# A feed-forward layer with fewer seven-product blocks, and matmul operands at one rest of 512 bytes

## The chip, the cores and the metric

The kernel runs on one core of one Trainium2 chip. The time is that of the device, in microseconds (us), as the median of several runs. TensorE multiplies matrices, VectorE (DVE) and ScalarE (ACT) do elementwise work, GpSimd (POOL) does small vector work and issues some DMAs, and SyncE (SP) issues most loads. Each engine works through its own queue in order, and semaphores tie the queues together.

## The reference

Two layers over 256 frames of width 2048, in float32. Layer 0 has a gated linear attention as its mixer, layer 1 a sparse attention; each adds its output to x, and then a gated feed-forward layer adds its own. What the change touches is the latter:

```python
def swiglu(h, w1, w3, w2):
    return (jax.nn.silu(h @ w1) * (h @ w3)) @ w2

def reference(x, ...):
    for i in range(DEPTH):                      # 2
        h = rmsnorm(x, norm_mix[i])
        ...
        x = x + y
        x = x + swiglu(rmsnorm(x, norm_ffn[i]), ffn_w1[i], ffn_w3[i], ffn_w2[i])
    return rmsnorm(x, norm_final)
```

w1 and w3 are 2048 x 5632, w2 is 5632 x 2048.

## The kernel before

**Products in three passes.** A float32 operand is split into a high part in the float32r format and the remainder: ScalarE casts the high part (`wh`, line 135), VectorE subtracts it (`wl`, line 136). A product is hi·wh + hi·wl + lo·wh, three matmuls of a 128 x 128 stationary tile and a 128 x 512 moving tile. The stationary tiles come from the activations, the moving ones from the weights. Weights arrive in tiles of 128 x 2048 (1 MB): four slices of 128 rows, by 512 columns. One such tile against one set of stationary tiles is 4 x 3 = 12 matmuls for 128 frames.

**The feed-forward layer** (`ffn`) works through 11 blocks of 512 columns of w1 and w3. With the 256 frames as two halves and the 2048 rows as two halves, one block is two products (with w1 and with w3) of a 2 x 2 block matrix. There are two ways to compute it:

- `plain` takes four products of half size for each of w1 and w3, eight in all, of 24 matmuls each: 192 matmuls. Its eight weight tiles come through the `raw` buffers (four of them) and are split once each. It uses the forms A11, F7 (the half difference a21 - a11), A12 and N22 (the negative of a22) of the activations.
- `pair` computes the two 2 x 2 products, which share their left matrix, with seven products of half size: 168 matmuls. For this it needs sums of weight tiles. Some are made by VectorE (`plus`, line 405), others by a DMA that adds what it loads to what lies in the buffer (`plus_dma`, line 408, issued on POOL's queue). Each product splits its two tiles anew: 14 casts and 14 subtractions. The tiles that are summed lie in the buffers v0, v1, v2 and g3, used in two sets that change places with `turn`, which is `b // 2 % 2` for block b; SP loads them at line 380. The activations have seven forms (fhA11, flA11, ... in the trace `fhA`, `fhF`, `fhN` and `fl` alike, numbers left out). There the lines are 393 for matmuls of a pair and 463 for those of a plain block.

The forms A11, F7, F5, A12, F6, F3 and N22 are made once for a layer, by `NormF`.

Both ways end in `done`, which makes silu(h w1) times h w3 for a half of the frames: it begins with a tanh on ScalarE (line 512). `split_t` then transposes the result (eight small matmuls a block, line 215) and splits it into the tiles `g0`, `g1` or `g2`, which are the stationary operands of the product with w2.

**The product with w2** is cut up. After blocks 1, 3, 5 and 7 the two finished blocks are put on a queue `down` as a generator `pieces`: eight steps, each with one tile of w2 and 24 matmuls (lines 489 to 491). The next block's generator yields eight times if it is a pair, twice if it is plain, and at each yield one step of `down` is issued. A generator that has given its eight steps is taken off `down` only when it is asked once more. So after block 2, 4, 6 and 8 the queue still holds an emptied generator, and it is dropped at the first yield of block 3, 5, 7 and 9. Since a block is a pair `if down`, blocks 2 to 9 are pairs, those with even numbers with eight pieces between their products, those with odd numbers with none. Blocks 0, 1 and 10 are plain. Blocks 8, 9 and 10 are multiplied with w2 in the step that follows (`residual`).

The other projections run through `gemm` (lines 201 to 203): stationary hh and hl, the normed activations, or `g` for the output projections; the last one ends in `gemm_tail` (lines 152 to 154), whose first wh and wl come from a pool of its own, the last one opened.

**Order.** The program is issued in the order of the code; each engine takes its instructions in that order. POOL's adding DMAs of a pair are issued one by one.

**Where tiles lie.** Pools take SBUF in the order in which they are opened: `cst` (small constants), `res` (x and g0 to g3), `wp` (raw, wh, wl), `cm`, `sm` (small tiles, 32 bytes each at the least), and then one pool for each stage, which holds hh and hl (`gp`, `dp`) or the forms and v0 to v2 (`fz0`, `fz1`), or the pool of the last step (`fp`). `cst` begins at byte 2176 of each partition. `cst` holds 32 + 512 + 288 bytes, `sm` 46 slots of 32 bytes, one of them an unused tile named pad. All other pools ahead of the stage's pool take multiples of 512 bytes.

Of the kernel before, what the change touches and what calls it, by code (L numbers as in the profile page):

```python
# [12 lines left out]
F32 = mybir.dt.float32  # L13
# [6 lines left out]
P = 128  # L20
# [3 lines left out]
NB = 512  # L24
# [31 lines left out]
def trunk(  # L56
# [9 lines left out]
    cst = ctx.enter_context(tc.tile_pool(name="cst", bufs=1))  # L66
# [3 lines left out]
    sm = ctx.enter_context(tc.tile_pool(name="sm", bufs=2))  # L70
# [13 lines left out]
            nc.sync.dma_start(x[t][n], x2[t, :, n * NB:(n + 1) * NB])  # L84


    neghalf = cst.tile([P, 8], F32, name="neghalf")
    nc.gpsimd.memset(neghalf, -0.5)
    warm = sm.tile([P, 8], F32, tag="warm", bufs=1, name="warm")
# [4 lines left out]
    cols = cst.tile([P, 72], F32, name="cols")  # L94


    sm.tile([P, 8], F32, tag="pad", bufs=1, name="pad")

    def gains(c0, srcs):

# [14 lines left out]
    def tick():  # L115

        while side:
            try:
                return next(side[0])
            except StopIteration:  # L120
                side.popleft()
# [9 lines left out]
    def split_w(raw, pool=wp):  # L131

        wh = pool.tile([P, 4, NB], F32R, tag="wh", bufs=3 if pool is wp else 1, name="wh")
        wl = pool.tile([P, 4, NB], F32R, tag="wl", bufs=3 if pool is wp else 1, name="wl")
        nc.scalar.copy(wh, raw)  # L135
        nc.vector.tensor_sub(wl, raw, wh.bitcast(F32))  # L136
        return wh, wl
# [221 lines left out]
    def hi_lo(i):  # L359
        g = res.tile([P, 2, 4, SEQ], F32R, tag=f"g{i}", name=f"g{i}")  # L360
        return g[:, 0], g[:, 1]

    def flush():
        while side:
            tick()


    def pair(nrm, wa, wb, c0, turn, done):

        def src(w, j, c):
            r = j * 1024 + c * 512
            return w[r:r + 512, c0:c0 + NB].rearrange("(k p) n -> p k n", p=P)

        def load(w, j, homes):
            o = []
            for c, (pool, tag, bufs) in enumerate(homes):
                raw = pool.tile([P, 4, NB], F32, tag=tag, bufs=bufs, name=tag)
                nc.sync.dma_start(raw, src(w, j, c))  # L380
                o.append(raw)
            return o

        def product(acc, raws, form, start, stop, then=None):
            for c in range(2):
                wh, wl = split_w(raws[c])
                if then is not None:
                    then(c)
                hi, lo = nrm.forms[form]
                for j in range(4):  # L390
                    k = 4 * c + j
                    for i, (l_, r_) in enumerate(((hi, wh), (hi, wl), (lo, wh))):
                        nc.tensor.matmul(acc, l_[:, k, :], r_[:, j, :], start=start and k == i == 0,  # L393
                                         stop=stop and k == 7 and i == 2, skip_group_check=not start)
                    if j % 2:
                        tick()

        def bank():
            return acc_p.tile([P, NB], F32, tag="acc", name="acc")

        def sums(tag):
            return nrm.pool.tile([P, NB], F32, tag=tag, bufs=1, name=tag)

        def plus(dst, other):
            return lambda c: nc.vector.tensor_add(dst[c], dst[c], other[c])  # L405

        def plus_dma(dst, w, j):
            return lambda c: nc.gpsimd.dma_start(dst[c], src(w, j, c), accum_op=ALU.add)  # L408

        fz = nrm.pool  # L410
        stream = [(wp, "raw", RAW)] * 2
        homes = [((fz, "v0", 1), (fz, "v1", 1)), ((fz, "v2", 1), (res, "g3", 1))]
        va = load(wa, 0, homes[turn])
        vb = load(wb, 0, homes[1 - turn])
        b1 = bank()
        product(b1, va, "A11", True, True, plus(va, vb))
        s1 = sums("s1")
        nc.scalar.copy(s1, b1)
        yield
        b2 = bank()  # L420
        product(b2, va, "F5", True, True, plus_dma(va, wb, 1))
        y = sums("y")
        nc.vector.tensor_sub(y, b2, s1)
        yield
        vc = load(wb, 1, stream)
        product(b2, vc, "F3", False, True, plus(vb, vc))
        yield
        b3 = bank()
        product(b3, va, "F6", True, True, plus_dma(va, wa, 1))
        w = sums("w")  # L430
        nc.vector.tensor_sub(w, b3, s1)
        yield
        product(b3, vb, "F7", False, True)
        nc.vector.tensor_add(w, w, b2)
        nc.vector.tensor_add(y, y, b3)
        yield
        vd = load(wa, 1, stream)
        product(b1, vd, "A12", False, True)
        done("11", b1)
        done("12", w)  # L440
        yield
        product(b3, va, "N22", False, True)
        nc.vector.tensor_sub(s1, s1, b3)
        done("21", s1)
        done("22", y)
        yield
        yield

    def plain(nrm, ws, c0, done):

        for q, w in zip("12", ws):
            acc = [acc_p.tile([P, NB], F32, tag="acc", name="acc") for _ in range(3)]
            for g in range(4):
                raw = wp.tile([P, 4, NB], F32, tag="raw", bufs=RAW, name="raw")
                nc.sync.dma_start(raw, w[g * NB:(g + 1) * NB, c0:c0 + NB].rearrange("(k p) n -> p k n", p=P))
                wh, wl = split_w(raw)
                for bank, form, start, stop in ((0, "A11", True, True), (1, "F7", True, True)) if g < 2 else \
                        ((0, "A12", False, True), (2, "N22", True, True)):
                    hi, lo = nrm.forms[form]
                    for j in range(4):  # L460
                        k = 4 * (g % 2) + j
                        for i, (l_, r_) in enumerate(((hi, wh), (hi, wl), (lo, wh))):
                            nc.tensor.matmul(acc[bank], l_[:, k, :], r_[:, j, :], start=start and k == i == 0,  # L463
                                             stop=stop and k == 7 and i == 2, skip_group_check=not start)
                        if j % 2:
                            tick()
                if g == 1:
                    s1 = nrm.pool.tile([P, NB], F32, tag="s1", bufs=1, name="s1")
                    nc.scalar.copy(s1, acc[0])
                    nc.vector.tensor_add(s1, s1, acc[1])  # L470
                    yield
            nc.vector.tensor_sub(s1, s1, acc[2])
            done("1" + q, acc[0])
            done("2" + q, s1)
# [24 lines left out]
    def ffn(layer, nrm):  # L499

        w1, w3, w2 = ffn_w1[layer], ffn_w3[layer], ffn_w2[layer]
        sc = {}
        parts = []
        down = deque()
        for b in range(DFF // NB):
            us = [None] * NT

            def done(q, v):
                t = int(q[0]) - 1
                if q[1] == "1":  # L510
                    us[t] = cm.tile([P, NB], F32, tag="u", name="u")
                    nc.scalar.activation(us[t], v, AF.Tanh, scale=sc["h"][:, t:t + 1])
                    nc.vector.scalar_tensor_tensor(us[t], us[t], 1.0, v, op0=ALU.add, op1=ALU.mult)
                else:
                    nc.vector.scalar_tensor_tensor(us[t], us[t], sc["r2"][:, t:t + 1], v, op0=ALU.mult, op1=ALU.mult)

            for slot, _ in enumerate(pair(nrm, w1, w3, b * NB, b // 2 % 2, done) if down else plain(nrm, (w1, w3), b * NB, done)):
                if b == 0 and slot == 0:
                    flush()
                    r = nrm.rstd()  # L520
                    sc["h"] = scaled(r, 0.5, "rh")
                    sc["r2"] = sm.tile([P, NT], F32, tag="r2", name="r2")
                    nc.gpsimd.tensor_tensor(sc["r2"], r, sc["h"], op=ALU.mult)
                while down:
                    try:
                        next(down[0])
                        break
                    except StopIteration:
                        down.popleft()
            hi, lo = hi_lo(b % 3)  # L530
            side.append(split_t(us, hi, lo))
            parts.append((hi, lo, b * NB))
            if b % 2 and b < 8:
                down.append(pieces(w2, parts))
                parts = []
        while down:
            for _ in down.popleft():
                pass
        return w2, parts
# [480 lines left out]
    with tc.tile_pool(name="gp", bufs=2) as gp:  # L1020
        n0.begin(gp)
        down = gla(n0, gp)
        flush()
    with tc.tile_pool(name="fz0", bufs=1) as fz:
        n1.begin(fz)
        residual(gla_w_out[0], down, n1.update)
        down = ffn(0, n1)
        flush()
    with tc.tile_pool(name="dp", bufs=2) as dp:
# [3 lines left out]
        down = dsa(n2, dp)  # L1033
        flush()
    with tc.tile_pool(name="fz1", bufs=1) as fz:
        n3.begin(fz)
        residual(dsa_w_out[0], down, n3.update)
        down = ffn(1, n3)
# [57 lines left out]
```

## Time and profile before

| | |
|---|---|
| median of 3 runs | 2426.34 us (2423.76 to 2428.74) |
| the profiled execution, in all | 2430.86 us |
| its span, first to last instruction | 2429.1 us |
| mean granted TensorE clock | 0.973 |
| DMA, mean over the span | 203 GB/s |
| read from HBM | 489.59 MB |

How to read it: the span is a little shorter than the time of the same execution, since it leaves out what lies before the first and after the last instruction. Busy times of matmuls overlap, since each begins before the one before it has ended; so the mean duration of one (some 390 ns) isn't its cost in a row of matmuls. The distance between two starts is. In a row of the timeline stand start and duration in us, engine, line, operation, output and inputs, and in brackets the engine's idle time before it and what ended it. In a row of the table of windows stand the stretch, its length, the busy time and the number of instructions of each engine, the granted clock, the share of the DMA engines and GB/s.

### The profile page before, as it was taken

To read this page: it belongs to the slowest core of one execution; us is meant where nothing else is said; L and a number is where in the kernel's file an instruction comes from. 1 tells how busy PE (TensorE), PEld (TensorE's weight loads), DVE (VectorE), ACT (ScalarE), POOL (GpSimd) and SP (SyncE) were. 2 spreads that over 40 slices of the span, in tenths; PEclk is the share of its full clock that TensorE was granted. 3 is DMA by queue.
4 is the path that set the end of the run, shared out by engine and by line. 5 is a ranking of instruction groups with operands and counts; after the bars stand their busy time and mean duration, and the time that the engine had idled before them with its cause. 6 is when DMAs were issued, how large, how long until landed. Compare 5 with 4: busy or idle time off the path is not lost.

```text
span 2429.1 us, 25156 instructions
## 1 busy us (share of the span) xinstructions
PE 2281.5 (94%) x10199; PEld 1857.5 (76%) x10199; DVE 1645.9 (68%) x1348; ACT 1183.5 (49%) x1053; POOL 112.8 (5%) x159
## 2 busy tenths in 40 slices
PE   9999999998897979989999999999988979889798
PEld 7888888876675867768888888888876867768687
DVE  6555456677886878865556655565786778878754
ACT  5545455454454445544444454454444545545443
POOL 0000000000000000000100000000000000000000
PEclk9999999999999989999999999999998999989899
DMA  8555466586877968775554545566677977779663
GB/s 280 164 174 180 148 219 232 172 233 194 232 242 207 286 184 222 229 205 187 182 173 139 191 157 174 174 219 212 176 235 201 293 182 225 230 190 311 138 218 112
DMA packets 254773, 493.36 MB, mean 203 GB/s; under 512 B 8200, under 2 KB 20832, under 8 KB 254528
## 3 DMA queue, kind: packets, MB, share of 16 engines
q1 hardware_dynamic: 219856, 423.33, 51.1%
q0 software_dynamic: 33792, 67.11, 16.0%
q8 instruction: 80, 1.31, 0.2%
q10 hardware_dynamic: 1008, 1.31, 0.2%
q14 instruction: 37, 0.30, 0.0%
HBM read 489.59 MB, written 2.12 MB: 202 GB/s over the span
## 4 chain that ended last, share of the span: by engine, by line
PE 59%; issue 21%; DMA 9%; DVE 8%; ACT 2%; POOL 1%; SPq 0%; POOLq 0%; ACTq 0%; DVEq 0%
PE acc L201 11%; PE acc L203 11%; PE acc L202 11%; PE acc L463 10%; DMA g<-in_ffn_w 6%; PE acc L393 6%; DVE wl L136 5%; DMA v<-in_ffn_w 3%; PE down L490 2%; ACT wh L135 2%; PE down L491 2%; PE down L489 2%; DVE v L405 1%; POOL v L408 1%; PE trq L827 0%
## 5 line engine op out<-in xcount | busy, mean ns | idle before, releaser
L192 DVE TENSOR_TENSOR wl<-raw,wh 128x2048 fp32r<-128x2048 f32 (+3 forms) x161 | 350.1, 2176 | 314.8 <-ACT wh L191 314.6
L136 DVE TENSOR_TENSOR wl<-raw,wh 128x2048 fp32r<-128x2048 f32 x179 | 409.5, 2289 | 184.7 <-ACT wh L135 184.7
L135 ACT CAST wh<-raw 128x2048 fp32r<-128x2048 f32 x179 | 342.3, 1912 | 392.6 <-PE down L491 144.3
L191 ACT CAST wh<-raw 128x2048 fp32r<-128x2048 f32 (+3 forms) x161 | 291.9, 1815 | 278.8 <-PE acc L203 217.7
L136 DVE TENSOR_TENSOR wl<-v,wh 128x2048 fp32r<-128x2048 f32 x120 | 272.7, 2286 | 83.1 <-ACT wh L135 83.1
L201 PE MATMUL acc<-wh,hh 128*128 128x512 f32 (+3 forms) x832 | 327.1, 393 | 0.0
L135 ACT CAST wh<-v 128x2048 fp32r<-128x2048 f32 x120 | 227.4, 1904 | 198.9 <-DMA v<-in_ffn_w 99.9
L203 PE MATMUL acc<-wh,hl 128*128 128x512 f32 (+3 forms) x832 | 318.4, 383 | 0.0
L202 PE MATMUL acc<-wl,hh 128*128 128x512 f32 (+3 forms) x832 | 317.0, 381 | 0.5 <-DVE wl L192 0.5
L393 PE MATMUL acc<-wh,fhF 128*128 128x512 f32 x512 | 216.5, 426 | 59.3 <-ACT wh L135 59.2
L393 PE MATMUL acc<-wl,fhF 128*128 128x512 f32 x512 | 216.0, 422 | 30.9 <-DVE wl L136 30.9
L490 PE MATMUL down<-wl,g 128*128 128x512 f32 x512 | 204.0, 398 | 9.3 <-DVE wl L136 9.3
L393 PE MATMUL acc<-wh,flF 128*128 128x512 f32 x512 | 212.2, 414 | 0.0
L491 PE MATMUL down<-wh,g 128*128 128x512 f32 x512 | 202.9, 396 | 0.0
L489 PE MATMUL down<-wh,g 128*128 128x512 f32 x512 | 200.3, 394 | 0.0
L203 PEld LDWEIGHTS acc<-wh,hl 128*128 128x128 f32 x832 | 156.2, 188 | 30.8
L202 PEld LDWEIGHTS acc<-wl,hh 128*128 128x128 f32 x832 | 156.6, 188 | 30.3 <-issue 1.7
L201 PEld LDWEIGHTS acc<-wh,hh 128*128 128x128 f32 x832 | 156.5, 188 | 28.9 <-issue 1.9
L393 PEld LDWEIGHTS acc<-wh,fhF 128*128 128x128 f32 x512 | 103.9, 205 | 91.2 <-ACT wh L135 68.3
L201 PE MATMUL acc<-wh,g 128*128 128x512 f32 x424 | 167.2, 394 | 0.0
L203 PE MATMUL acc<-wh,g 128*128 128x512 f32 x424 | 165.5, 390 | 0.0
L202 PE MATMUL acc<-wl,g 128*128 128x512 f32 x424 | 165.4, 390 | 0.0
(282 smaller groups left out, 3608.6 us busy)
## 6 DMA issues: line engine op xcount, KB each, us to landing
raw<-in_ffn_w SPq DMA_DIRECT2D x200, 1024.0 KB, 5.8
v<-in_ffn_w SPq DMA_DIRECT2D x48, 1024.0 KB, 6.6
v<-in_ffn_w POOLq DMA_DIRECT2D x48, 1024.0 KB, 9.4
raw<-in_dsa_w_in SPq DMA_DIRECT2D x48, 1024.0 KB, 5.1
raw<-in_gla_w_in SPq DMA_DIRECT2D x40, 1024.0 KB, 5.1
raw<-in_gla_w_out SPq DMA_DIRECT2D x16, 1024.0 KB, 5.2
g<-in_ffn_w SPq DMA_DIRECT2D x16, 1024.0 KB, 6.7
g<-in_ffn_w POOLq DMA_DIRECT2D x16, 1024.0 KB, 13.3
```

Of the source, the lines that this page charges most:

```text
L135: nc.scalar.copy(wh, raw)
L136: nc.vector.tensor_sub(wl, raw, wh.bitcast(F32))
L191: a = nc.scalar.copy(wh[:, sl, :n], raw[:, sl, :n])
L192: v = nc.vector.tensor_sub(wl[:, sl, :n], raw[:, sl, :n], wh[:, sl, :n].bitcast(F32))
L201: nc.tensor.matmul(acc[t][:, :n], hi[:, k, ts_], wh[:, k, :n], start=start, stop=False)
L202: nc.tensor.matmul(acc[t][:, :n], hi[:, k, ts_], wl[:, k, :n], start=False, stop=False)
L203: nc.tensor.matmul(acc[t][:, :n], lo[:, k, ts_], wh[:, k, :n], start=False, stop=last)
L393: nc.tensor.matmul(acc, l_[:, k, :], r_[:, j, :], start=start and k == i == 0, stop=stop and k == 7 and i == 2, skip_group_check=not start)
L463: nc.tensor.matmul(acc[bank], l_[:, k, :], r_[:, j, :], start=start and k == i == 0, stop=stop and k == 7 and i == 2, skip_group_check=not ...
L489: nc.tensor.matmul(acc[t], hi[:, k, ts_], wh[:, k, :], start=start, stop=False)
L490: nc.tensor.matmul(acc[t], hi[:, k, ts_], wl[:, k, :], start=False, stop=False)
L491: nc.tensor.matmul(acc[t], lo[:, k, ts_], wh[:, k, :], start=False, stop=last)
```

## The change

The choice between `pair` and `plain` no longer asks whether `down` holds a generator but goes by the number of the block: 2, 4, 6 and 8 are pairs, and 0, 1, 3, 5, 7, 9 and 10 are plain. In addition an unused tile of 64 bytes is put first into `cst`, and the unused tile of `sm` grows from 32 to 96 bytes, so that tiles behind the first move by 64 bytes and tiles behind both by 128.

```diff
@@ -84,6 +84,7 @@
             nc.sync.dma_start(x[t][n], x2[t, :, n * NB:(n + 1) * NB])
 
 
+    cst.tile([P, 16], F32, name="pad")
     neghalf = cst.tile([P, 8], F32, name="neghalf")
     nc.gpsimd.memset(neghalf, -0.5)
     warm = sm.tile([P, 8], F32, tag="warm", bufs=1, name="warm")
@@ -94,7 +95,7 @@
     cols = cst.tile([P, 72], F32, name="cols")
 
 
-    sm.tile([P, 8], F32, tag="pad", bufs=1, name="pad")
+    sm.tile([P, 24], F32, tag="pad", bufs=1, name="pad")
 
     def gains(c0, srcs):
 
@@ -514,7 +515,7 @@
                 else:
                     nc.vector.scalar_tensor_tensor(us[t], us[t], sc["r2"][:, t:t + 1], v, op0=ALU.mult, op1=ALU.mult)
 
-            for slot, _ in enumerate(pair(nrm, w1, w3, b * NB, b // 2 % 2, done) if down else plain(nrm, (w1, w3), b * NB, done)):
+            for slot, _ in enumerate(pair(nrm, w1, w3, b * NB, b // 2 % 2, done) if b in range(2, 9, 2) else plain(nrm, (w1, w3), b * NB, done)):
                 if b == 0 and slot == 0:
                     flush()
                     r = nrm.rstd()
```

## The prediction

> **What bounds the kernel now.** I read the page first, then the ACT timeline for marks that part the blocks of the feed-forward layer, then the table of windows between these marks.
>
> ```profile
> span 2429.1 us, 25156 instructions
> ...
> PE 2281.5 (94%) x10199; PEld 1857.5 (76%) x10199; DVE 1645.9 (68%) x1348; ACT 1183.5 (49%) x1053; POOL 112.8 (5%) x159
> ```
>
> TensorE is busy for 94% of the span, so the kernel is bound by matmuls almost everywhere. The question is where the other 6% lies, and what one matmul costs.
>
> My mark is the first tanh of a block (line 512, reading an accumulator). That of block 1 in layer 0 is
>
> ```profile
> 461.40 0.69 ACT L512 ACTIVATE u<-acc,rh 128x512 f32<-128x512 f32 x1 [0.84 <-PE acc L463]
> ```
>
> and the windows run from such a mark to another. Layer 0 is the rows from 416.60 to 1092.36, layer 1 those from 1694.08 on.
>
> ```profile
> core 0: us, PE busy (x) PEld busy (x) DVE busy (x) ACT busy (x) POOL busy (x), PEclk, DMA share, GB/s
> 416.60:461.40 44.80, 44.80 (x201) 36.81 (x200) 24.85 (x19) 18.95 (x15) 0.00 (x0) 1.00 0.60 188
> 461.40:549.46 88.06, 86.23 (x381) 70.49 (x380) 66.92 (x43) 43.28 (x27) 5.41 (x4) 1.00 0.75 212
> 549.46:625.52 76.06, 62.96 (x260) 49.57 (x258) 55.33 (x36) 34.90 (x22) 5.17 (x4) 0.93 0.77 212
> 625.52:696.59 71.07, 65.54 (x285) 52.74 (x286) 61.41 (x39) 38.94 (x25) 5.19 (x4) 1.00 0.86 247
> 696.59:844.48 147.89, 129.03 (x545) 102.28 (x544) 116.67 (x75) 73.61 (x47) 10.37 (x8) 0.97 0.81 226
> 844.48:993.51 149.03, 131.12 (x545) 104.60 (x544) 117.10 (x75) 73.81 (x46) 10.38 (x8) 0.94 0.81 229
> 993.51:1066.60 73.09, 60.83 (x249) 47.98 (x248) 56.20 (x37) 34.99 (x23) 5.19 (x4) 0.93 0.71 186
> 1066.60:1092.36 25.76, 25.76 (x117) 21.05 (x116) 18.60 (x15) 14.34 (x11) 0.00 (x0) 1.00 0.60 207
> ...
> 1694.08:1781.34 87.26, 86.10 (x381) 70.49 (x380) 66.91 (x43) 43.30 (x27) 5.23 (x4) 1.00 0.75 214
> 1781.34:1930.95 149.61, 133.02 (x545) 106.19 (x544) 116.93 (x75) 73.85 (x47) 10.37 (x8) 0.93 0.80 227
> 1930.95:2080.80 149.85, 132.89 (x545) 106.31 (x544) 116.91 (x75) 73.82 (x46) 10.37 (x8) 0.93 0.79 224
> 2080.80:2229.34 148.54, 132.24 (x545) 105.60 (x544) 117.11 (x75) 74.05 (x46) 10.37 (x8) 0.92 0.81 227
> 2229.34:2304.09 74.75, 62.23 (x249) 49.12 (x248) 56.27 (x37) 34.97 (x22) 5.18 (x4) 0.91 0.70 184
> 2304.09:2329.73 25.64, 25.64 (x117) 21.03 (x116) 18.67 (x15) 14.34 (x12) 0.00 (x0) 1.00 0.62 208
> ```
>
> Three kinds of block stand here. A plain block (first row, 192 matmuls and 8 transposes) has TensorE busy for all of its 44.80 us at full clock. A seven-product pair with the eight pieces of w2 between its products (second row, from block 1 into block 2) loses under 2 us of 88.06. A seven-product pair alone, block 3 (third row), loses 13 us, and the granted clock falls to 0.93. Block 9 alone (993.51 and 2229.34) loses 12 us in each layer. So the pairs without pieces, blocks 3, 5, 7, 9, hold the idle time. What happens in them:
>
> ```profile
> 589.96 1.90 ACT L135 CAST wh<-v 128x2048 fp32r<-128x2048 f32 x1 [5.68 <-DMA v<-in_ffn_w]
> 600.86 1.90 ACT L135 CAST wh<-g 128x2048 fp32r<-128x2048 f32 x1 [9.00 <-DMA g<-in_ffn_w]
> ```
> ```profile
> 591.91 1.22 PE L393 MATMUL acc<-wh,fhF 128*128 128x512 f32 x2 [6.88 <-ACT wh L135]
> ```
>
> The cast waits for the adding DMA of line 408, and TensorE waits for the cast. The pair has a chain of its own (cast, split, adding DMA, cast again), and with only 24 matmuls between two links nothing covers it. With pieces in between, it is covered.
>
> **The change, part by part.**
>
> *Blocks 3, 5, 7, 9 of both layers become plain.* Each goes from 7 products of 24 matmuls (168) to 192, so 8 x 24 = 192 matmuls are added. Per block, six casts and six splits go, four adds on VectorE, four adding DMAs on POOL's queue; SP issues eight loads in both forms. Of these, VectorE's splits are
>
> ```profile
> L136 DVE TENSOR_TENSOR wl<-v,wh 128x2048 fp32r<-128x2048 f32 x120 | 272.7, 2286 | 83.1 <-ACT wh L135 83.1
> ```
>
> 6 x 2.286 = 13.7 us a block, and the casts and adds come on top. I cost all of it at nothing: in the pair alone it lies beside TensorE's work or inside the chain whose wait is already in the old rows, and a plain block keeps VectorE busy for 24.85 of 44.80 us only. What counts is TensorE's time between marks, and three transitions make up the new layer.
>
> Plain into pair (blocks 1-2, 3-4, 5-6, 7-8): the trace has this one, 88.06 and 87.26, mean 87.66. The later ones issue in the same order. Each pair's first tiles are the buffers that the pair before released earliest, and now a whole plain block lies between; the loads of a pair stand on SP's queue behind the plain block's eight loads, as they do for block 2, whose first cast of such a tile waited for TensorE and not for a DMA:
>
> ```profile
> 475.13 1.91 ACT L135 CAST wh<-v 128x2048 fp32r<-128x2048 f32 x1 [2.16 <-PE acc L463]
> ```
>
> Pair into plain (2-3, 4-5, 6-7, 8-9): not in the trace. From mark to mark it has 24 matmuls of the last product, 72 of three pieces, 84 of the plain block, and 8 transposes. The row from 1066.60 (25.76; 25.64 in layer 1) is the same without the pieces and lost nothing. So 25.70 + 72 x 0.2269 (the pace is below) = 42.0. From below the bound is these matmuls, 41; from above the row into a pair alone, 76.06. I take 42.0, since the nearest row has a plain block behind a pair and TensorE busy throughout. The plain block's loads have four buffers and go out in the order in which they are used.
>
> Plain into plain (9-10): 44.80.
>
> New layer, mark of block 1 to mark of block 10: 4 x 87.66 + 4 x 42.0 + 44.80 = 563.4. Old: the rows of layer 0 add up to 630.96, of layer 1 to 635.65. Saved: 67.5 + 72.2 = **139.8 us**. The matmuls that are added are in this sum: they are 192 x 0.2288 = 44, so the idle time and lower clock that go are worth some 184.
>
> What is late next is the pair itself: block 2 keeps one wait of 1.8 us for its adding DMA, which is in the 87.66.
>
> *The pads.* The pools lie one behind the other: constants, residents (x, g), weights (wh, wl), work tiles, small tiles, then the layer's pool with hh or the fh/fl forms. Everything is a multiple of 512 bytes except the constants (832) and the small tiles (46 slots of 32 bytes, 1472 = 2 x 512 + 448). So g stands at the same rest of 512 as wh and wl, and hh, fh, fl stand 64 bytes behind. The pads make these pools 896 and 1536: all at one rest, and by the base of 2176 bytes that rest is 0. Does the rest matter? Four stretches of the PE timeline, 128x512 matmuls with nothing between:
>
> ```profile
> 380.21 0.39 PE L201 MATMUL acc<-wh,g 128*128 128x512 f32 x1
> ...
> 395.41 0.39 PE L202 MATMUL acc<-wl,g 128*128 128x512 f32 x1
> ```
> ```profile
> 410.16 0.39 PE L463 MATMUL acc<-wh,fhA 128*128 128x512 f32 x1
> ...
> 421.60 0.39 PE L463 MATMUL acc<-wh,flA 128*128 128x512 f32 x1
> ```
> ```profile
> 156.37 0.39 PE L201 MATMUL acc<-wh,hh 128*128 128x512 f32 x1
> ...
> 165.98 0.39 PE L201 MATMUL acc<-wh,hh 128*128 128x512 f32 x1
> ```
> ```profile
> 2404.16 0.39 PE L152 MATMUL acc<-wh,g 128*128 128x512 f32 x1
> ...
> 2406.73 0.39 PE L154 MATMUL acc<-wh,g 128*128 128x512 f32 x1
> ```
>
> The 67 steps with g take 15.20 us, 0.2269 each. The 50 with the forms take 11.44, the 42 with hh 9.61: 0.2288 each. The last has g again, but wh comes from the last pool, so that the rests differ the other way: 11 steps in 2.57, 0.2336. One line, one shape, one stationary tile, and the pace goes with the rests. So equal rests are worth about 1.9 ns a matmul. How many:
>
> ```profile
> L201 PE MATMUL acc<-wh,hh 128*128 128x512 f32 x736 | 296.8, 403 | 0.0
> ```
>
> Three such lines with hh make 2208; the forms after the change have 8 pairs x 168 + 14 plain x 192 = 4032. 6240 x 1.9 ns = **12 us**. No trace shows both at rest 0, so I keep both ends: no gain (0), and everything at the worst pace seen. The second is 6240 x 4.8 ns + 2880 matmuls with g x 6.7 ns = 49 us lost.
>
> The Trainium skill, TensorE: Matmul & The Clock Gate, Part 2 (what happens when you issue a matmul), gives TensorE two independent read ports and says that loading the next weights does not take read bandwidth from the running matmul; by that rule the pads are worth nothing. The steps of 0.2336 against 0.2269 speak against it, at least for how the two rests stand to each other.
>
> *Sum.* The profiled run took 2430.9 us in all (span 2429.1). 2430.9 - 139.8 - 12 = 2279. The median shown, 2426.3, lies 4.5 below that run, so the forecast is **2275 us**.
>
> **The rivals.**
>
> 1. *The rests are worth nothing.* Loads of weights and reads of the moving operand do not disturb one another, and the 0.2288 comes from something else in these stages. For it: 2 ns is little, and hh and the forms differ from g in more than their address. Against: the tail's 0.2336. 2275 + 12 = 2287.
> 2. *Rest 0 is a bad one.* Both operands on it meet at every matmul. 2275 + 12 + 49 = 2336. Against: g and wh agree now, at another rest, and that is the fastest pace.
> 3. *The adding DMA is late in pairs 4, 6, 8 too.* In the pair alone TensorE waited 6.88 us for it. Were one such wait to come back in each of six pairs: 6 x 6.9 = 41, 2316. Against: block 2 stands behind a plain block already and waits 1.8.
> 4. *Slower: the plain block starves behind a pair.* Place: SP's queue, where its loads stand behind the pair's and the pieces' loads. Price: if it lost as much as the pair alone loses now, only the added matmuls would be left, +44, and with rival 1 that is 2426 + 44 = 2470. It turns the sign as soon as a plain block takes 17 us more than 44.8 (139.8 / 8). Against: 44.80 and 25.76 show no wait, at a DMA share of 0.60.
>
> That the change does not do what it says can be followed in the code: blocks 2, 4, 6, 8 are those after which a queue of pieces was filled (after blocks 1, 3, 5, 7), and the emptied queue, which made `down` true for one block more, is no longer asked.
>
> **How the numbers follow.** Forecast 0.65, rival 1 0.20, rival 2 0.06, rival 3 0.06, rival 4 0.03. The forecast's own spread is about 14 us either way: up to 2 us a transition for the six pairs that are new behind a plain block, and the pace by a third of a nanosecond over some 6240 matmuls. With rival 1, at 2287 and 10 us of that spread, the range is 2261 to 2297, and leaves out rivals 2 to 4 with 0.15. A change within 0.2%, about what a measurement of this kernel can tell from none, has 0.01, slower than that 0.03, faster 0.96.
>
> **What would show it.** The matmul count of the page goes from 10199 to about 10391. Line 408 falls from 64 adding DMAs to 32. The windows between marks alternate 88 and 42, with clock 1.00. A step with hh or a form takes 0.2269; if it stays at 0.2288, rival 1 holds; if g rises to 0.2336, rival 2. Waits of line 135 on the adding DMA over 5 us in blocks 4, 6, 8 would be rival 3. The forecast is wrong if a plain block after a pair takes clearly more than 45 us.

## The result, and the profile after

The changed kernel takes **2287.3 us** (median of 4 runs, 2285.86 to 2289.09) against 2427.06 us before, a ratio of 0.9426 (95% interval 0.941 to 0.9442). The forecast was 2275, the range 2261 to 2297. The profiled execution took 2286.86 us in all, its span 2284.7.

The page of the changed kernel, first lines:

```profile
span 2284.7 us, 25267 instructions
## 1 busy us (share of the span) xinstructions
PE 2255.5 (99%) x10391; PEld 1865.6 (82%) x10391; DVE 1471.6 (64%) x1260; ACT 1101.8 (48%) x1013; POOL 71.2 (3%) x127
```

192 matmuls more, as counted, and TensorE busy for 99% instead of 94%: 144.4 us of span are gone although work was added. The table of windows between the first tanh of the blocks, layer 0 (b1-b2, then b2-b3 and so on up to b9-b10), and the last three of layer 1's transitions into a pair:

```profile
core 0: us, PE busy (x) PEld busy (x) DVE busy (x) ACT busy (x) POOL busy (x), PEclk, DMA share, GB/s
...
459.42:547.70 88.28, 85.95 (x381) 70.36 (x380) 66.88 (x43) 43.39 (x28) 5.42 (x4) 1.00 0.75 209
547.70:589.44 41.74, 41.74 (x189) 34.58 (x188) 28.19 (x22) 20.18 (x15) 0.00 (x0) 1.00 0.76 262
589.44:676.88 87.44, 85.66 (x381) 70.36 (x380) 66.85 (x43) 43.38 (x27) 5.17 (x4) 1.00 0.75 214
676.88:718.62 41.74, 41.74 (x189) 34.57 (x188) 28.20 (x22) 20.19 (x14) 0.00 (x0) 1.00 0.77 258
718.62:806.21 87.59, 85.76 (x381) 70.36 (x380) 66.89 (x43) 43.39 (x28) 5.19 (x4) 1.00 0.74 211
806.21:847.95 41.74, 41.74 (x189) 34.58 (x188) 28.20 (x22) 20.18 (x15) 0.00 (x0) 1.00 0.76 260
847.95:937.48 89.53, 87.56 (x381) 71.56 (x380) 67.15 (x43) 43.37 (x27) 5.19 (x4) 0.98 0.70 191
937.48:979.22 41.74, 41.74 (x189) 34.57 (x188) 28.20 (x22) 20.19 (x14) 0.00 (x0) 1.00 0.60 195
979.22:1023.70 44.48, 44.48 (x201) 36.81 (x200) 24.90 (x19) 18.98 (x15) 0.00 (x0) 1.00 0.59 190
...
1752.37:1841.49 89.12, 87.29 (x381) 71.50 (x380) 67.15 (x43) 43.37 (x27) 5.18 (x4) 0.98 0.76 214
1841.49:1883.23 41.74, 41.74 (x189) 34.57 (x188) 28.19 (x22) 20.18 (x14) 0.00 (x0) 1.00 0.74 248
1883.23:1970.73 87.50, 85.68 (x381) 70.37 (x380) 66.90 (x43) 43.39 (x28) 5.19 (x4) 1.00 0.76 212
```

Every stretch into a plain block (41.74) and between two plain blocks (44.48) has TensorE busy all the time. Every stretch into a pair lacks some 2 us, and in two of eight the granted clock falls to 0.98 on top (89.53, 89.12). The mean of the eight is 88.05. Nearly all of their idle time is one wait. (The lines of the changed kernel are numbered one higher than before: its 394 is 393 there.) It stands here from the waits of the whole run and from the PE and ACT timelines of block 4:

```profile
PE acc L394 <- DVE wl L137: 14.5, 8, 1.8
```
```profile
652.30 0.50 PE L394 MATMUL acc<-wl,fhF 128*128 128x512 f32 x1 [1.78 <-DVE wl L137]
```
```profile
648.01 1.91 ACT L136 CAST wh<-v 128x2048 fp32r<-128x2048 f32 x1 [6.66 <-DMA v<-in_ffn_w]
```

Eight waits, one a pair, 14.5 us in all (before, TensorE waited 41.2 us for splits and 76.8 us for casts in the pairs). The cast of the second tile of the F6 product waits for the second adding DMA, the split waits for the cast, the matmul for the split.

And the pace, from the PE timeline of a plain block, first and last row of 50 steps:

```profile
408.63 0.39 PE L464 MATMUL acc<-wh,fhA 128*128 128x512 f32 x1
...
419.96 0.39 PE L464 MATMUL acc<-wh,flA 128*128 128x512 f32 x1
```

11.33 us, 0.2266 a step, where the same matmuls took 0.2288 before. So the pads did what was forecast to the matmuls, and yet the time is that of the rival in which they are worth nothing (2287). The experiments had to say how both can be.

### The profile page after: what moved, and what is told of

Its sections match the earlier page's. It is cut to its first block, busy times and chain, and to the rows that moved or that the text cites. A ratio compares the mean times of both kernels' runs of the same rounds, so it can differ in the third digit from the quotient of the medians.

```text
span 2284.7 us, 25267 instructions
## 1 busy us (share of the span) xinstructions
PE 2255.5 (99%) x10391; PEld 1865.6 (82%) x10391; DVE 1471.6 (64%) x1260; ACT 1101.8 (48%) x1013; POOL 71.2 (3%) x127
## 4 chain that ended last, share of the span: by engine, by line
PE 69%; issue 20%; DMA 5%; DVE 3%; ACT 1%; POOL 1%; SPq 0%; POOLq 0%; ACTq 0%
PE acc L464 18%; PE acc L202 12%; PE acc L204 12%; PE acc L203 12%; PE acc L394 5%; DMA g<-in_ffn_w 3%; DMA v<-in_ffn_w 3%; PE down L490 2%; PE down L491 2%; PE down L492 2%; DVE wl L137 1%; ACT wh L136 1%; PE tr L216 1%; POOL v L409 0%; PE trq L828 0%
## 5 line engine op out<-in xcount | busy, mean ns | idle before, releaser
L137 DVE TENSOR_TENSOR wl<-raw,wh 128x2048 fp32r<-128x2048 f32 x211 | 483.2, 2290 | 265.8 <-ACT wh L136 264.9
L136 ACT CAST wh<-raw 128x2048 fp32r<-128x2048 f32 x211 | 403.7, 1913 | 475.8 <-PE acc L464 193.7
L492 PE MATMUL down<-wh,g 128*128 128x512 f32 x512 | 199.2, 389 | 0.0
L491 PE MATMUL down<-wl,g 128*128 128x512 f32 x512 | 199.2, 389 | 0.0
L490 PE MATMUL down<-wh,g 128*128 128x512 f32 x512 | 198.0, 389 | 0.0
L464 PE MATMUL acc<-wh,fhA 128*128 128x512 f32 x448 | 175.9, 393 | 0.2
L464 PE MATMUL acc<-wl,fhA 128*128 128x512 f32 x448 | 174.7, 390 | 0.0
L464 PE MATMUL acc<-wh,flA 128*128 128x512 f32 x448 | 174.5, 390 | 0.0
L137 DVE TENSOR_TENSOR wl<-v,wh 128x2048 fp32r<-128x2048 f32 x60 | 136.9, 2287 | 41.7 <-ACT wh L136 41.7
L136 ACT CAST wh<-v 128x2048 fp32r<-128x2048 f32 x60 | 114.7, 1912 | 86.5 <-PE acc L464 31.2
L394 PE MATMUL acc<-wl,fhF 128*128 128x512 f32 x256 | 102.0, 398 | 14.5 <-DVE wl L137 14.5
```

The costliest lines, as they stand in the source:

```text
L490: nc.tensor.matmul(acc[t], hi[:, k, ts_], wh[:, k, :], start=start, stop=False)
L491: nc.tensor.matmul(acc[t], hi[:, k, ts_], wl[:, k, :], start=False, stop=False)
L492: nc.tensor.matmul(acc[t], lo[:, k, ts_], wh[:, k, :], start=False, stop=last)
```

## The experiments

Each is timed against the kernel before, on the same chip. "After" is the changed kernel, 2287.3 us. The runs fall into four groups, in which the kernel before took 2427.03, 2427.83, 2427.43 and 2428.97 us; so a difference between two experiments of different groups is good to about 2 us.

**e1: the blocks alone.** After without the pads:

```diff
-    cst.tile([P, 16], F32, name="pad")
-    sm.tile([P, 24], F32, tag="pad", bufs=1, name="pad")
+    sm.tile([P, 8], F32, tag="pad", bufs=1, name="pad")
```

> Blocks 3, 5, 7, 9 plain, pads as before. If the pads are worth what the pace of the matmuls says (6240 steps that fall from 0.2288 or so to 0.2269), this is some 12 us above the changed kernel: 2299 us, 2294 to 2303, with steps of 0.229 on hh and the forms. If the pads are worth nothing and the blocks alone made the gain: 2287 us.

Measured: 2287.64 us, ratio 0.9422 (0.9409 to 0.9435). The pads are worth nothing in this schedule: the expectation of 2299 fell, and its alternative of 2287 came true. But the traces show the pace as forecast: a plain block's steps take 0.229 here. The windows, block 2 to 6 of layer 0:

```profile
550.16:592.12 41.96, 41.96 (x189) 34.59 (x188) 28.20 (x22) 20.19 (x15) 0.00 (x0) 1.00 0.75 257
592.12:679.95 87.83, 86.17 (x381) 70.50 (x380) 66.93 (x43) 43.30 (x28) 5.17 (x4) 1.00 0.75 212
679.95:721.91 41.96, 41.96 (x189) 34.58 (x188) 28.21 (x22) 20.19 (x15) 0.00 (x0) 1.00 0.76 258
721.91:808.68 86.77, 86.12 (x381) 70.50 (x380) 66.90 (x43) 43.32 (x28) 5.19 (x4) 1.00 0.75 215
```

Where only matmuls set the time, e1 is slower (41.96 against 41.74). Into a pair it is *faster*: the mean of the eight is 87.18 against 88.05. Taken over the span, 2286.7 and 2284.7: after gains 5.6 us outside the feed-forward blocks and 3.3 in the plain ones, and loses 8 x 0.87 = 7.0 in the pairs. In these, TensorE is idle for 15.2 us in after and for 6.5 in e1 (the length of the eight stretches less their busy time). In e1 the wait for the split falls to this:

```profile
PE acc L393 <- DVE wl L136: 6.1, 5, 1.8
```

The clock is not what differs: it fell in one pair of e1 too (89.92 us, clock 0.98), and without the stretches in which it fell the means are 86.79 and 87.63. What is longer is the adding DMA. POOL's timeline in block 8, where the difference is largest, first of e1, then of after:

```profile
894.66 1.30 POOL L408 DMA_DIRECT2D v<-in_ffn_w  x1 [7.55 <-DMA v<-in_ffn_w]
908.04 1.29 POOL L408 DMA_DIRECT2D v<-in_ffn_w  x1 [12.09 <-DMA v<-in_ffn_w]
```
```profile
892.00 1.30 POOL L409 DMA_DIRECT2D v<-in_ffn_w  x1 [7.71 <-DVE y L424]
907.19 1.29 POOL L409 DMA_DIRECT2D v<-in_ffn_w  x1 [13.89 <-DMA v<-in_ffn_w]
```

The third adding DMA is issued when the second has landed: 13.4 us later in e1, 15.2 us in after. From issue to landing the second one takes 13.65 us in the mean of the eight pairs of e1 (13.0 to 14.8), 14.46 in after (14.2 to 14.9). TensorE's wait hangs on exactly this one: in e1 TensorE idles for 0.1 us in the three pairs where it takes up to 13.1 us, and for 1.7 and 2.0 us in the two where it takes over 14.

**e2: the pads alone,** on the kernel before (its choice of blocks kept).

> Pads alone, blocks as before. By the pace: 5 us outside the feed-forward blocks and 2 to 7 us in them, where the pairs without pieces wait for DMAs and can't use a faster matmul: 2415 to 2420 us. If the pads are worth nothing: 2427 us.

Measured: 2431.25 us, ratio 1.0019 (1.0008 to 1.0031): not faster, rather a little slower, and outside both expectations. The first stretch up to block 1's mark is shorter by about as much as in after (459.20 against 461.40 us). Over the whole span 5.1 us are gained outside the stretches from block 1's mark to block 10's, and 5.5 lost in them.

**e3: one piece earlier.** After, with one of the two yields behind the last product of a pair moved between F3 and F6:

```diff
         product(b2, vc, "F3", False, True, plus(vb, vc))
         yield
+        yield
         b3 = bank()
...
         done("22", y)
         yield
-        yield
```

> The changed kernel, with one of the two pieces behind the last product of a pair moved ahead of the F6 product. Theory: each pair's one wait (2.2 us, eight of them, two of which also halved the clock for 3.4 us) is that the two adding DMAs, one after the other, take longer than the 72 matmuls between the splits of F5 and F6; 24 more cover it. Then 8 x 2.2 + 2 x 1.7 = 21 us go: 2266 us, 2264 to 2272. Rival: the wait comes from the DMAs' queue and moves on to the next product that needs an added tile: 2285 to 2290 us.

Measured: **2266.75 us**, ratio 0.9338 (0.9325 to 0.935), as the theory had it, and the fastest of all kernels here. Its windows from block 2 to block 5:

```profile
550.80:587.10 36.30, 36.30 (x165) 30.07 (x164) 24.45 (x19) 18.27 (x13) 0.00 (x0) 1.00 0.76 261
587.10:677.90 90.80, 90.80 (x405) 74.94 (x404) 70.78 (x46) 45.53 (x28) 5.17 (x4) 1.00 0.76 220
677.90:714.20 36.30, 36.30 (x165) 30.07 (x164) 24.45 (x19) 18.27 (x13) 0.00 (x0) 1.00 0.76 260
```

The two together are 127.10 (24 matmuls have changed sides) against 129.2 to 131.3 in after, TensorE is busy throughout, and the clock stays at 1.00. The cast still waits for the DMA (4.15 us in block 4), but TensorE has a piece to work on meanwhile.

**e8: the same without the pads.**

> The kernel with the piece moved ahead (2266.75 us), without the pads. The pads shorten a step by some 2 ns in the traces, yet the blocks alone took 2287.64 us against 2287.3 with pads. Theory: the pads' 12 us are real on TensorE, but with them the second adding DMA of a pair takes 14.3 us instead of 13.3, and the wait for it eats the gain; where nothing waits for it, the pads are worth their 12 us: 2278 us, 2274 to 2282, with steps of 0.229. Rival: the pace of the records doesn't reach the time, pads are worth nothing anywhere: 2265 to 2269.

Measured: 2277.32 us, ratio 0.9388 (0.9371 to 0.9404). The same two kinds of stretch, 36.51 and 91.31 against 36.30 and 90.80 in e3:

```profile
553.35:589.86 36.51, 36.51 (x165) 30.08 (x164) 24.44 (x19) 18.25 (x13) 0.00 (x0) 1.00 0.77 259
589.86:681.17 91.31, 91.31 (x405) 75.08 (x404) 70.89 (x46) 45.41 (x29) 5.17 (x4) 1.00 0.75 218
```

So where TensorE does not idle for the adding DMA, the pads are worth 2277.32 - 2266.75 = 10.6 us, close to the 12 of the forecast. The rival, that the pace doesn't reach the time, is out. The second adding DMA takes 13.3 us here and 14.3 in e3: the difference is there also where it costs nothing.

**e5, e6, e7: other distances of the two rests.** Moving operands and g stay at rest 0, the pad of the small tiles alone is changed:

```diff
-    sm.tile([P, 24], F32, tag="pad", bufs=1, name="pad")
+    sm.tile([P, 8], F32, tag="pad", bufs=1, name="pad")    # e5: hh and the forms at 448
+    sm.tile([P, 40], F32, tag="pad", bufs=1, name="pad")   # e6: at 64
+    sm.tile([P, 88], F32, tag="pad", bufs=1, name="pad")   # e7: at 256
```

> The changed kernel with the small tiles' pad back at 32 bytes: wh, wl and g at rest 0, hh and the forms at rest 448, 64 bytes behind, as before, but at other rests. If the difference of the two rests counts: steps of 0.2288 to 0.2300 with hh and the forms, 0.2269 with g. If rest 0 of the moving operand is what counts: 0.2269 everywhere. Time 2287 to 2290 either way, as far as the adding DMA sets the pairs.

> The pad of the small tiles at 160 bytes: hh and the forms at rest 64, wh, wl and g at 0, so the stationary operand is 64 bytes ahead, as in the last projection's first tile before, which ran at 0.2336. If the difference counts, with its sign: 0.2336 on hh and the forms; the plain blocks go from 44.4 to 45.7 us, and the time by 5400 steps outside the pairs' waits x 6.7 ns = 36 us to 2323 us. If only equal or unequal counts: 0.2288 and 2290 us.

> Small tiles' pad at 352 bytes: hh and the forms at rest 256, the others at 0. Seen so far: equal rests 0.2270, stationary 64 behind 0.229, 64 ahead 0.2333. If the cost falls with the distance, steps of 0.227 and 2285 us; if being ahead by any amount costs the same, 0.2333 and 2307 us.

Fifty steps of a plain block in e6, first and last row:

```profile
413.69 0.39 PE L464 MATMUL acc<-wl,fhA 128*128 128x512 f32 x1
...
425.36 0.39 PE L464 MATMUL acc<-wh,fhA 128*128 128x512 f32 x1
```

11.67 us, 0.2334 a step. In the same way e5 has 0.2290 and e7 0.2268.

| hh and forms against wh, wl | a step, us | second adding DMA, us | time, us |
|---|---|---|---|
| equal (after) | 0.2266 | 14.46 | 2287.3 |
| 64 behind (e5) | 0.2290 | 13.36 | 2285.17 |
| 64 ahead (e6) | 0.2334 | 13.46 | 2306.96 |
| 256 ahead (e7) | 0.2268 | 14.26 | 2287.44 (one run) |

It is the distance with its sign that counts, not equality as such, and not rest 0: the kernel before had 64 behind at other rests, with the same 0.229. In all these kernels the tiles of these matmuls are multiples of 512 bytes long, so that only this distance changes; whether a shorter period than 512 would describe it as well was not tried. e6 is slower, but by 20 us and not by the 36 I had expected: its plain stretches are longer (42.46 against 41.74 us), but the mean stretch into a pair is 87.51 against 88.05, since slower steps there take up what was waiting (TensorE idles for at most 0.5 us in each). e5 came out 2 us below what I expected and below after, although its steps are slower: its mean stretch into a pair is 86.7 us, with the shorter adding DMA and no fall of the clock.

**e10: v2 alone at another rest.** What makes the second adding DMA longer? In after all its targets stand at rest 0.

```diff
-        homes = [((fz, "v0", 1), (fz, "v1", 1)), ((fz, "v2", 1), (res, "g3", 1))]
+        homes = [((fz, "v0", 1), (fz, "v1", 1)), ((res, "g3", 1), (fz, "v2", 1))]
+        fz.tile([P, 16], F32, tag="p0", bufs=1, name="p0")
```

> The changed kernel, with v2 alone moved off rest 0 (to 64) and made the second tile of its set, so in blocks 2 and 6 the second adding DMA goes to v2 (rest 64), in blocks 4 and 8 to v1 (rest 0). Theory: the second adding DMA takes 14.3 us instead of 13.4 because the tile that it adds to stands at rest 0: then 13.4 in blocks 2 and 6, 14.3 in 4 and 8, and some 4 us less in all, 2283 us. Rival: it is the faster matmuls around it, or the rests of the others: 14.3 in all blocks, 2287 us.

Measured: 2286.94 us, ratio 0.9428 (0.9402 to 0.9454); the second adding DMA takes 13.9 to 14.5 us in all eight pairs, with the target at rest 64 as at 0. My theory fell. Over all runs the long ones (14.2 to 14.5 in the mean: after, e3, e7, e10) are those with steps of 0.227, the short ones (13.3 to 13.7: e1, e5, e6, e8) those with slower steps. What the traces do show is that an adding DMA is long where loads run beside it: in after, the first of each pair has 0.2 to 0.4 MB of SP's loads beside it and takes 8.5 to 9.1 us, the second has 3.1 to 3.4 MB and takes 14.2 to 14.9. Counted from the start of the second one, the loads that SP issues around it come 0.1 to 0.2 us earlier in the mean in after than in e1. That would fit loads that a faster TensorE releases sooner and that share the DMA engines with the adding DMA. But per microsecond they move the same in both (0.22 MB), so the bytes alone do not tell cause from effect, and no run here shows the cause by itself: it stays open.

**e4 and e11: what a pair alone waits for.** The kernel before, first without the adding DMAs in blocks 3, 5, 7 and 9, then without VectorE's four adds there too. Both leave out sums that the result needs, and serve for timing alone:

```diff
-    def pair(nrm, wa, wb, c0, turn, done):
+    def pair(nrm, wa, wb, c0, turn, done, adds=True):
...
-            return lambda c: nc.gpsimd.dma_start(dst[c], src(w, j, c), accum_op=ALU.add)
+            return (lambda c: nc.gpsimd.dma_start(dst[c], src(w, j, c), accum_op=ALU.add)) if adds else None
...
-            return lambda c: nc.vector.tensor_add(dst[c], dst[c], other[c])                       # e11 alone
+            return (lambda c: nc.vector.tensor_add(dst[c], dst[c], other[c])) if adds else None   # e11 alone
...
-... pair(nrm, w1, w3, b * NB, b // 2 % 2, done) if down ...
+... pair(nrm, w1, w3, b * NB, b // 2 % 2, done, b % 2 == 0) if down ...
```

> The kernel before, with the four adding DMAs left out in the pairs without pieces (blocks 3, 5, 7, 9), so these blocks are computed from tiles to which nothing was added. Theory: the chain of adding DMAs is what keeps such a pair waiting; without it the pair runs at the pace of its 168 matmuls, so 18 to 25 us a block go: 2427 - 8 x 22 = 2250 us, 2235 to 2280. Rival: the first loads are late, since the pair uses the same buffers for its first sum as the pair before it; then at least half of the idle time stays: above 2330 us.

> As the run without the adding DMAs in blocks 3, 5, 7, 9 (2332.7 us, above what I expected), and in these blocks without the four adds of weight tiles on VectorE too: 4 x 2.28 us a block less there. What is left of the idle time is some 14 us per two blocks. Theory: VectorE is what the pair alone waits for next: 14 splits and 4 adds of weight tiles are 41 us, and with the rest of its work some 49, against 39 us of matmuls. Then most of the 14 us go with the adds: 7 to 12 us a block, 2240 to 2280 us. Rival: the loads of tiles are late, since a set of buffers is used twice running: 2320 to 2333 us.

Measured: e4 2332.7 us, ratio 0.9609 (0.9592 to 0.9625); e11 2312.68 us, 0.9511 (0.9495 to 0.9527). So the adding DMAs cost a pair alone (2427.03 - 2332.7) / 8 = 11.8 us, and the sums on VectorE some 2.5 us more. Both theories gave times that were too low. e4 lies where its rival has it (above 2330), and e11 lies between its theory and its rival; my second theory, that VectorE is the next bound, holds for a small part only. TensorE's waits of the whole run in e4:

```profile
PE acc L393 <- ACT wh L135: 33.2, 21, 2.0
...
PE acc L393 <- DVE wl L136: 15.3, 10, 1.6
```

The 118 us of before (76.8 and 41.2) are down to 48.5, and none is longer than 2.0. In e11 a cast of such a block still waits for TensorE to give back one of the three wh buffers, and TensorE then waits for the cast:

```profile
582.05 1.90 ACT L135 CAST wh<-v 128x2048 fp32r<-128x2048 f32 x1 [0.83 <-PE acc L393]
```
```profile
584.01 0.73 PE L393 MATMUL acc<-wh,fhF 128*128 128x512 f32 x2 [1.99 <-ACT wh L135]
```

Even with nothing to add, a pair alone is thus slower than its 168 matmuls. The rival of both runs, loads that come late, is not borne out by their traces: in the feed-forward blocks every cast that waits for a DMA, seven in e4 and eight in e11, stands in a pair with pieces and waits for an adding DMA, none for a load of SP.

**e9: pairs everywhere, with four pieces each.** After, with blocks 2 to 9 as pairs, pieces at four of a pair's eight yields, and the sets of buffers changing places at every pair:

```diff
-... pair(nrm, w1, w3, b * NB, b // 2 % 2, done) if b in range(2, 9, 2) else plain(...)
+... pair(nrm, w1, w3, b * NB, b % 2, done) if b in range(2, 10) else plain(...)
...
-                while down:
+                while down and slot in (1, 2, 3, 5):
```

> All of blocks 2 to 9 as pairs again (168 matmuls instead of 192 in four blocks of a layer), but each with four pieces, two ahead of F6 and two ahead of N22, and with the two sets of buffers changing places at every pair. Per two blocks 528 matmuls, 121 us, against 90.8 + 36.3 = 127.1 with the piece moved ahead. VectorE has some 62 us of work in such a block, against 61 on TensorE. Theory: what a pair alone waited for was the adding DMA (12 us, by the run without it) and VectorE (the rest), so with half the cover each both are just covered: 62 to 65 us a block, 2255 to 2285 us. Rival: the loads that the changed order of buffers asks for are late: over 2290 us.

Measured: 2330.45 us, ratio 0.9605 (0.9588 to 0.9622). The theory (2255 to 2285) fell, and the time is on the rival's side (over 2290). Two blocks of it; the cast before F6's second half in one; and the start of a pair, where a cast waits for VectorE's sum and the sum for a tile that SP loads:

```profile
606.42:743.50 137.08, 127.96 (x545) 102.52 (x544) 116.85 (x75) 73.88 (x46) 10.37 (x8) 0.98 0.85 246
```
```profile
652.35 1.90 ACT L136 CAST wh<-v 128x2048 fp32r<-128x2048 f32 x1 [8.30 <-DMA v<-in_ffn_w]
```
```profile
617.14 2.29 DVE L406 TENSOR_TENSOR v<-v,v 128x2048 f32<-128x2048 f32 x1 [1.05 <-DMA v<-in_ffn_w]
619.55 1.91 ACT L136 CAST wh<-v 128x2048 fp32r<-128x2048 f32 x1 [3.05 <-DVE v L406]
```

137 us for two blocks against 127.1 in e3. The cast waits 8.30 us for the adding DMA, and VectorE is busy for 117 of 137 us. In 14 of the 16 pairs the first sum on VectorE waits 0.35 to 2.48 us for a tile that SP loads, so the rival's late loads are there, beside the rest; how much of the time is theirs was not tried. 24 matmuls fewer for two blocks don't pay for all that. Eight pieces in one pair and none in a plain block is the better use of the same pieces.

## Why the prediction was right, and where it was not

**Where the idle time lay** was right: blocks 3, 5, 7, 9 without pieces. As plain blocks they lose nothing.

**Pair into plain, 42.0; plain into plain, 44.80.** Measured 41.74 and 44.48: the terms without the pads' gain were right to 0.1 us. e1, without pads, has 41.96.

**Plain into pair, 87.66.** In e1 the mean of eight is 87.18, 0.5 below the term.

**The pads, 12 us, taken as a gain of the whole.** Here the prediction's sum failed. The pace was right (0.2266 for a forecast of 0.2269), and so was its size where nothing else binds (10.6 us by e3 and e8). What failed is that I added it to a row with a wait in it. The 1.8 us for the adding DMA "is in the 87.66", I wrote, and took it as fixed. It isn't: with the pads the second adding DMA lasts longer by 0.8 us in the mean, the stretch into a pair goes from 87.18 to 88.05, and 7.0 of the 8.9 us that the pads gain elsewhere are lost again. Of the forecast 12 us, 8 x 252 steps x 1.9 ns = 3.8 lay in the stretches into a pair, which lost 7.0 instead: 10.8 us short there, 0.7 more than forecast elsewhere. For the profiled run the forecast was 2279, and 2291.1 without the pads. e1, without them, took 2288.8, 2.3 less; after took 2286.9, so the pads were worth 1.9 us there and not 12. Together that is the 7.8 us by which the profiled run is over 2279.

**The other 4.5 us** are the step from the profiled run to the median. I let the profiled run's distance to the median of before stand for the changed kernel too; there, the profiled run (2286.86) lies at the median.

**Rival 1** has the time that was measured, 2287, for a reason that the traces rule out: the steps did become faster. The measured time lies 12 us above the forecast, near the end of its own spread of 14 us. Of these, 12 are for pairs that are slower by up to 2 us each, but the reason given there was the plain block in front of them and not the pads. That the 2287 of this rival is hit is luck: what the pads lost at the adding DMA happens to be nearly what they gained elsewhere. **Rival 2** is out (rest 0 is no worse than another), **rival 4** too: no plain block starves. **Rival 3** is there in small: no wait of 6.9 us comes back, but every pair has one of 1.8 us, and two of eight also lose clock by it.

**The cause of the idle time** was told too simply. The adding DMA is the greater part (11.8 us a block by e4), but "that chain" isn't all: 2.5 us go to VectorE's sums, which I had costed at nothing, and more to the casts and their buffers. The forecast did not suffer by it, since it took the blocks' time from rows of the trace.

**The rule of the Trainium skill** on two independent read ports (TensorE: Matmul & The Clock Gate, Part 2): e6 against after disagrees with the use that the prediction made of it, that the pads are worth nothing. The same matmuls take 0.2334 or 0.2266 us by nothing but the distance of two addresses. That the loading of weights and the reading of the moving operand get in each other's way would fit, but no run here shows what is slower inside a step.

## What to carry to other kernels

A gain of pace is only a gain where nothing waits: before adding it up, mark the stretches that a DMA ends, and look whether that DMA keeps its length; here it did not. A wait of 2 us that is left over after a change can be a matter of order: here one piece of unrelated work moved by one place was worth 20 us, more than the pads. And where two ways to compute a block trade matmuls for dependent steps, the one with fewer matmuls won here only with enough unrelated work to put between the steps; half the cover for twice the blocks lost.

## What the runs showed of the hardware that was not expected

The pace of this kernel's 128 x 512 matmul stream in float32r depends on where the stationary and the moving operand stand to each other, here counted modulo 512 bytes: 0.2266 us with equal rests, 0.2268 with the stationary one 256 ahead, 0.229 with it 64 behind, 0.2334 with it 64 ahead. Other distances were not tried. The granted clock fell to half for 3.4 us in two of the eight pairs of the changed kernel, each with a wait of TensorE of only some 2 us, and these two stretches were longer by 1.6 and 2.0 us than the 87.5 of the others nearest to them. The other six pairs have the same wait and kept the clock.
